# Expert stage of a diffusion block: each block's scatter-add is queued one iteration later on GpSimd, and the gathered rows are held in two tiles by column halves

## The chip, the cores and the metric

The program runs on one core of a Trainium2 chip. The metric is the device time of one execution in microseconds. TensorE does the matrix products, ScalarE and VectorE convert and scale, GpSimd issues the indirect DMAs (gather and scatter) and makes fp16 copies, SyncE issues the plain loads. In the profile they are called PE (PEld for its weight loads), ACT, DVE, POOL and SP.

## The reference, cut to what matters

One layer of a hybrid backbone: three groups of heads side by side (gated MLP, attention, gated recurrence), an output projection, and then a mixture of experts over 2048 tokens. Only the last part is touched here. Every token goes to two of 32 experts; an expert is a gated MLP with weights w1 and w3 (1024 x 512) and w2 (512 x 1024), and its output is added to the token's row, scaled by the token's gate:

```
out = (silu(xb @ w1[e]) * (xb @ w3[e])) @ w2[e]
x   = x + g2 * segment_sum(out[dest] * gate, token)
```

## The kernel before

`moe` (L1345 and on) works through 47 blocks of token rows. The experts are ranked by load; rank r has room for `CAPS[r]` groups of 64 rows, so a block is **full** (128 rows, 29 of them) or **half** (64 rows, 18 of them). The list `seq` takes a large, a middle and a small expert in turn, so the early part of the stage has more blocks per expert (more products for each weight loaded) than the late part.

The order of the instructions on PE, ACT, DVE and POOL is the order of the Python code (`manual_schedule`); each engine takes its own in order, and what is written first goes first. Iteration i does, in this order:

- `fetch(i + 4)`: on POOL, two small register loads and up to two loads of the index table (L1371, L1375).
- `gather(i + 2)`: on POOL, an indirect DMA that brings the rows of block i+2 into `xg` (L1443).
- first quarter of `gate_up(i)`: PE multiplies two 128-column chunks of x by w1 and w3, high part and residue (L1488, L1490) and then the fp16 weight residue (L1493 for half blocks, L1496 for full ones).
- `hidden(i - 1)`: PE transposes the activation `ac` of the block before into `pat` (L1469); ACT writes its rounded part `ah`, DVE the residue `al` (in `ah` itself for half blocks), POOL the fp16 copy `ab` (L1437).
- second quarter of `gate_up(i)`, then `rows(i + 1)`: PE transposes `xg` into the PSUM tile `pxt` (L1453), and twice, for columns 0 to 3 and 4 to 7 of the chunks, ACT writes `xh` (L82), DVE `xl` (L85; in `xh` for half blocks), POOL `xb` (L1437).
- third and fourth quarter of `gate_up(i)`, the activation (`sg`, `ac`), then `down(i - 1)`: PE multiplies `ah`, `al` by w2 (L1488, L1490) and `ab` by w2's residue (L1493, L1496) into `py`; ACT and DVE make `ysb`, the scaled output (L1544, L1545, L1547); POOL scatters it with an add into `out` (L1549).

The scatter is the last POOL instruction of an iteration, ahead of the next iteration's index load, gather and `ab`:

```
nc.gpsimd.indirect_dma_start(
    out=a["out"], out_offset=bass.IndirectOffsetOnAxis(ap=idx[r][:n, j, 0:1], axis=0),
    in_=y[:n], in_offset=None, compute_op=OP.add)
```

Between these steps the weights come in 384 pieces of 512 KB through five buffers `wstage` (L1406, on SP). ACT (L1416) makes the rounded part of a piece and DVE (L1417) its residue, which frees the buffer for the next load. `ahead` places these conversions by a fixed count of time for each quarter, so their place among the other ACT and DVE instructions is fixed in the program; up to 15 pieces of w1 and w3 and 7 of w2 lie ready ahead of PE. `ysb` has one buffer, `xg`, `xh`, `xl` and `xb` two, the index tile seven.

Of the kernel before, what the change touches and what calls it, by code (L numbers as in the profile page):

```python
# [10 lines left out]
F32 = mybir.dt.float32  # L11
F32R = mybir.dt.float32r
F16 = mybir.dt.float16
I32 = mybir.dt.int32
U8 = mybir.dt.uint8
AF = mybir.ActivationFunctionType
OP = mybir.AluOpType
# [4 lines left out]
P = 128  # L22
D = 1024
KT = D // P
# [50 lines left out]
class Kern:  # L75
# [1271 lines left out]
    def moe(self):  # L1347
        nc, tc, a = self.nc, self.tc, self.a
# [7 lines left out]
        seq = [(r, j) for r in order for j in range(nb(r))]  # L1356
        half = lambda r, j: 2 * j + 1 == CAPS[r]
        with ExitStack() as es:
            pool = es.enter_context(tc.tile_pool(name="moe", bufs=2, reuse_waits="tile"))
# [1 line left out]
            g2 = pool.tile([P, D], F32, name="g2", bufs=1)  # L1361
            nc.sync.dma_start(g2, self.mod_d[0:1, 5 * D:6 * D].to_broadcast([P, D]))
            nc.vector.tensor_scalar(g2, g2, 1.0 / UP, None, op0=OP.mult)
            idx, XG, XT, AC, AT, W = {}, {}, {}, {}, {}, {}

            def fetch_idx(r):
                e = nc.gpsimd.value_load(self.perm[0:1, r:r + 1], min_val=0, max_val=E_ - 1)
                n = CAPS[r] // 2
                t = pool.tile([P, 4, 2], I32, name="idx", bufs=7)
                if n:  # L1370
                    nc.gpsimd.dma_start(t[:, :n],  # L1371
                                        tabv[bass.ds(e, 1), :n * P].rearrange("o (j p) c -> p (o j) c", p=P))
                idx[r] = t
                if CAPS[r] % 2:
                    nc.gpsimd.dma_start(t[:64, n:n + 1], tabv[bass.ds(e, 1), n * P:n * P + 64]  # L1375
                                        .rearrange("o (j p) c -> p (o j) c", p=64))
# [24 lines left out]
            def pump():  # L1401
                p = next(gen, None)
                if p is None:
                    return
                st = pool.tile([P, 1024], F32, name="wstage", bufs=self.STG)
                nc.sync.dma_start(st if p[0][1] == "w2" else st.rearrange("p (k f) -> p k f", k=2), p[1])  # L1406
                dq.append((p[0], st))
# [13 lines left out]
            def need(r, w, k):  # L1421
                while (r, w, k) not in W:
                    split_next()
                    clock[0] = max(clock[0] - self.PACE, -self.PACE)
                return W[r, w, k]
# [3 lines left out]
            def ahead(t):  # L1429

                clock[0] = min(clock[0] + t, 3 * self.PACE)
                while clock[0] >= self.PACE and dq and free[kind(dq[0][0][1])] > 0:
                    split_next()
                    clock[0] -= self.PACE

            def half16(o, x):
                nc.gpsimd.tensor_scalar(o, x, -65504.0, 65504.0, op0=OP.max, op1=OP.min)  # L1437
# [9 lines left out]
            def rows(i):  # L1447

                n = 64 if half(*seq[i]) else P
                xg = XG.pop(i)  # L1450
                pt = ps.tile([P, KT, n], F32, name="pxt")
                for k in range(KT):
                    nc.tensor.transpose(pt[:, k], xg[:n, k * P:(k + 1) * P], self.ident[:n, :n])  # L1453
                h = pool.tile([P, KT, P], F32R, name="xh", bufs=2)
                l = h[:, :, 64:] if n == 64 else pool.tile([P, KT, P], F32R, name="xl", bufs=2)
                b = pool.tile([P, KT, P], F16, name="xb", bufs=2)
                for s in range(2):
                    ss = slice(4 * s, 4 * s + 4)
                    self.split(h[:, ss, :n], l[:, ss], pt[:, ss])
                    half16(b[:, ss, :n], h[:, ss, :n])  # L1460
                XT[i] = h, l, b

            def hidden(i):

                n = 64 if half(*seq[i]) else P
                ac = AC.pop(i)
                pt = ps.tile([P, 4, n], F32, name="pat")
                for k in range(4):
                    nc.tensor.transpose(pt[:, k], ac[:n, k * P:(k + 1) * P], self.ident[:n, :n])  # L1469
                h = pool.tile([P, 4, P], F32R, name="ah", bufs=1)  # L1470
                l = h[:, :, 64:] if n == 64 else pool.tile([P, 4, P], F32R, name="al", bufs=1)
                b = pool.tile([P, 4, P], F16, name="ab", bufs=1)
                self.split(h[:, :, :n], l, pt)
                half16(b[:, :, :n], h[:, :, :n])
                AT[i] = h, l, b

            def mm(i, out, x, ws, cs, last):


                small = half(*seq[i])  # L1480
                h, l, b = x
                first = small and (cs[0] // 2) % 2 == 1
                for low in ((True, False) if first else (False, True)):
                    for m, c in enumerate(cs):
                        for s in range(2):
                            w = ws[s][m][low]
                            if not low:
                                nc.tensor.matmul(out[s], h[:, c], w, start=(c == 0), stop=(first and c == last))  # L1488
                                if not small:
                                    nc.tensor.matmul(out[s], l[:, c], w, start=False, stop=False)  # L1490
                            elif small:
                                z = slice(64 * s, 64 * s + 64)
                                nc.tensor.matmul(out[s][z], b[:, c, :64], w, start=False, stop=False,  # L1493
                                                 tile_position=(0, 64 * s))
                            else:
                                nc.tensor.matmul(out[s], b[:, c], w, start=False, stop=(c == last))  # L1496

            def gate_up(i):

# [27 lines left out]
            def down(i):  # L1527
                r, j = seq[i]
                x = AT.pop(i)
                py = ps.tile([P, 2, 512], F32, name="py")  # L1530
                out = py[:, 0], py[:, 1]
                for k in (0, 2):
                    pcs = [need(r, "w2", k + m) for m in range(2)]
                    ws = [[[v[:, s * 512:(s + 1) * 512] for v in pc] for pc in pcs] for s in range(2)]
                    mm(i, out, x, ws, (k, k + 1), 3)
                    if j == nb(r) - 1:
                        free["w2"] += 2
                    ahead(6.5 if half(r, j) else 12)
                y = pool.tile([P, D], F32, name="ysb", bufs=1)
                src = pf = py.rearrange("p a b -> p (a b)")  # L1540
                n = P
                if half(r, j):
                    n = 64
                    nc.scalar.activation(y[:64], pf[64:], AF.Copy)  # L1544
                    nc.vector.tensor_tensor(y[:64], pf[:64], y[:64], op=OP.add)  # L1545
                    src = y
                nc.vector.scalar_tensor_tensor(y[:n], src[:n], idx[r][:n, j, 1:2].bitcast(F32), g2[:n],  # L1547
                                               op0=OP.mult, op1=OP.mult)
                nc.gpsimd.indirect_dma_start(  # L1549
                    out=a["out"], out_offset=bass.IndirectOffsetOnAxis(ap=idx[r][:n, j, 0:1], axis=0),  # L1550
                    in_=y[:n], in_offset=None, compute_op=OP.add)

            def fetch(i):
                if i < len(seq) and seq[i][1] == 0:
                    fetch_idx(seq[i][0])

            N = len(seq)
            with tc.manual_schedule(engines=ENGINES):
                for i in range(4):
                    fetch(i)  # L1560
                for _ in range(self.STG):
                    pump()
                gather(0)
                gather(1)
                rows(0)
                for i in range(N):
                    fetch(i + 4)
                    if i + 2 < N:
                        gather(i + 2)
                    g = gate_up(i)  # L1570
                    next(g)
                    if i:
                        hidden(i - 1)
                    next(g)
                    if i + 1 < N:
                        rows(i + 1)
                    for _ in g:
                        pass
                    if i:
                        down(i - 1)  # L1580
                hidden(N - 1)
                down(N - 1)
        self.overflow()

    def overflow(self):
# [151 lines left out]
```

## Time and profile before

| | us |
|---|---|
| median of 3 runs | 2933.82 |
| range of the runs | 2923.05 to 2935.71 |
| the profiled execution | 2931.78 |
| its span, first to last instruction | 2930.1 |
| expert stage in it, first weight load to last instruction | 2055 to 2930 |

The span is that of the program's own instructions; 1.7 us lie around it. Busy shares say how full an engine is, waits say what it stood for; a wait is told as "who <- whom", with its total, how often and the longest. `PEclk` is the granted TensorE clock: 1.0 is 2.4 GHz and 0.5 is 1.2 GHz.

### The profile page before, as it was taken

The page shows a single profiled execution, that of the slowest core. Times are in us where ns is not written, and L with a number is a line of the kernel's source. Part 1 is how long each engine was busy: PE and PEld are TensorE (multiplying, and loading weights), DVE is VectorE, ACT ScalarE, POOL GpSimd, SP SyncE. Part 2 cuts the span into 40 slices and gives each one's busy share as a digit, 9 for nine tenths or more (in the row PEclk, how much of TensorE's full clock was granted, in tenths as well). Part 3 has the DMA queues.
Part 4 walks back from the last instruction along what each step waited for, and adds up shares of the span by engine and source line. Part 5 has one row for each costly group of instructions (what it writes and reads, how often), then busy time and mean ns, then how long its engine had stood idle before and what let it go on. Part 6 is the DMA issues. An engine that isn't in the chain of part 4 may idle for free. (4 is left out here: it accounts for less than half of the span.)

```text
span 2930.1 us, 39701 instructions
## 1 busy us (share of the span) xinstructions
PE 2598.4 (89%) x13276; PEld 1918.9 (65%) x13276; DVE 2021.8 (69%) x3049; ACT 1547.4 (53%) x2599; POOL 1740.4 (59%) x1374
## 2 busy tenths in 40 slices
PE   6888888679978999999999999997798989898886
PEld 3778887568865666666666667776465555564553
DVE  3777767674445666667777654777678778878885
ACT  3344333312224777778887882222456656666664
POOL 3334333547775777778888885554455555555453
PEclk9999999789998999999999999998899999998998
DMA  7221223133321111121101006432789889999995
GB/s 283 95 78 65 80 87 105 46 104 99 103 81 60 60 58 50 57 67 34 31 30 30 17 10 200 151 131 76 268 264 285 281 265 308 307 299 290 290 296 156
DMA packets 208686, 409.99 MB, mean 140 GB/s; under 512 B 27568, under 2 KB 82224, under 8 KB 208352
## 3 DMA queue, kind: packets, MB, share of 16 engines
q1 hardware_dynamic: 194976, 367.52, 37.6%
q0 software_dynamic: 13504, 39.93, 6.3%
q8 instruction: 105, 1.72, 0.2%
q14 instruction: 101, 0.83, 0.1%
HBM read 336.00 MB, written 71.37 MB: 139 GB/s over the span
## 5 line engine op out<-in xcount | busy, mean ns | idle before, releaser
L963 POOL TENSOR_TENSOR pl<-pf,ph 128x512 f16<-128x512 f32 x512 | 683.9, 1345 | 155.9 <-ACT ph L960 131.8
L900 DVE TENSOR_REDUCE mx<-pmx 128x1 f32<-128x512 f32 (+1 forms) x640 | 403.3, 636 | 206.7 <-PE pmx L898 199.9
L959 ACT ACTIVATE pf<-s 128x512 f32<-128x512 f32 x576 | 344.5, 598 | 177.7 <-PE s L956 158.8
L1417 DVE SCALAR_TENSOR_TENSOR w13l<-wstage,w13h 128x1024 f16<-128x1024 f32 x256 | 319.1, 1279 | 35.3 <-ACT w13h L1416 30.7
L960 ACT ACTIVATE ph<-s 128x512 fp32r<-128x512 f32 x576 | 342.0, 594 | 0.0
L1549 POOL DMA_INDIRECT out_dram<-ysb,idx x47 | 117.4, 2499 | 365.7 <-DVE ysb L1547 357.8
L976 PE MATMUL p<-ph,one 128*128 128x512 f32 x576 | 333.1, 578 | 0.0
L1416 ACT ACTIVATE w13h<-wstage 128x1024 fp32r<-128x1024 f32 x256 | 261.5, 1051 | 90.6 <-DMA wstage<-in_w_dram 58.6
L1488 PE MATMUL ph<-w13h,xh 128*128 128x512 f32 x752 | 289.5, 431 | 20.1 <-DVE ac L1524 6.8
L898 PE MATMUL pmx<-k,q 128*128 128x512 f32 (+1 forms) x640 | 242.3, 380 | 8.1 <-DVE mx L900 3.9
L956 PE MATMUL s<-qB,kB 65*128 65x512 f32 x576 | 231.5, 402 | 6.4 <-POOL kB L947 6.4
L955 PE MATMUL s<-q,k 128*128 128x512 f32 x576 | 230.3, 400 | 0.0
L974 PE MATMUL p<-ph,VV 128*128 128x512 f32 x576 | 226.9, 394 | 0.0
L975 PE MATMUL p<-pl,V 128*128 128x512 f16 x576 | 224.2, 389 | 1.2 <-ACT ec L984 1.1
L1488 PEld LDWEIGHTS ph<-w13h,xh 128*128 128x128 f32 x752 | 139.5, 191 | 77.1 <-issue 15.4
L1490 PE MATMUL ph<-w13h,xl 128*128 128x512 f32 x464 | 184.9, 398 | 0.0
L536 PE MATMUL pa<-Q,kz 128*128 128x128 f32 x896 | 127.3, 302 | 62.4 <-DVE Asc L561 50.0
L1417 DVE SCALAR_TENSOR_TENSOR w2l<-wstage,w2h 128x1024 f16<-128x1024 f32 x128 | 158.3, 1262 | 30.3 <-ACT w2h L1416 20.7
L1437 POOL TENSOR_SCALAR xb<-xh 128x512 f16<-128x512 f32 (+1 forms) x94 | 168.1, 1819 | 15.9 <-ACT xh L82 15.9
L1488 PE MATMUL py<-w2h,ah 128*128 128x512 f32 x376 | 156.3, 463 | 10.5 <-ACT ah L82 5.3
L536 PEld LDWEIGHTS pa<-Q,kz 128*128 128x128 f32 x896 | 119.7, 214 | 68.7 <-issue 44.0
L975 PEld LDWEIGHTS <-V 128*128 128x128 f16 x576 | 54.9, 95 | 149.9 <-issue 139.2
(378 smaller groups left out, 6562.2 us busy)
## 6 DMA issues: line engine op xcount, KB each, us to landing
wstage<-in_w_dram SPq DMA_DIRECT2D x384, 512.0 KB
wm<-in_w_mod_dram SPq DMA_DIRECT2D x48, 512.0 KB
xtok<-in_x_tok_dram SPq DMA_DIRECT2D x34, 512.0 KB
hf<-h_d SPq DMA_DIRECT2D x19, 512.0 KB
xT<-in_xT_dram SPq DMA_DIRECT2D x18, 512.0 KB
h_d<-xT SPq DMA_DIRECT2D x18, 512.0 KB
qf<-qT_d SPq DMA_DIRECT2D x64, 128.0 KB
out_dram<-xn SPq DMA_DIRECT2D x16, 512.0 KB
```

The costliest lines, as they stand in the source:

```text
L536: nc.tensor.matmul(pa[:, hd], self.kz[l][:, hd, s], Q[:, hd, s], start=True, stop=True)
L898: nc.tensor.matmul(pm[:, :m], q2[:, t * P:(t + 1) * P], kk[:, j * 512:j * 512 + m], start=True, stop=True)
L900: nc.vector.tensor_reduce(mx[:, t, j:j + 1], pm[:, :m], axis=AX.X, op=OP.max)
L956: nc.tensor.matmul(s, kB[:, g, j], qB, start=False, stop=True)
L959: nc.scalar.activation(pf, s, AF.Exp, scale=0.125)
L960: nc.scalar.activation(ph, s, AF.Exp, scale=0.125)
L963: subs.append(lambda: e.tensor_tensor(pl, pf, ph, op=OP.subtract))
L975: nc.tensor.matmul(p[1], V1[:, g, j].rearrange("p s d -> p (s d)"), pl, **f)
L976: nc.tensor.matmul(p[1], one, ph, start=False, stop=(j == NT - 1))
L1416: nc.scalar.activation(h, st, AF.Copy, scale=UP)
L1417: nc.vector.scalar_tensor_tensor(l, st, UP, h, op0=OP.mult, op1=OP.subtract)
L1488: nc.tensor.matmul(out[s], h[:, c], w, start=(c == 0), stop=(first and c == last))
```

## The change

The scatter becomes a function of its own, `scatter(i)`. In iteration i, block i-2 is scattered, right after `hidden(i - 1)` and ahead of the second quarter of `gate_up(i)`; it was block i-1 at the end of the iteration. `ysb` gets two buffers and the index tile eight. `rows` makes for each half of the chunks its own tiles `xh`, `xl`, `xb` (four buffers of half the size), and `mm` takes chunk c from tile c // 4. The PSUM tile `pxt` stays one tile, and the order of ACT, DVE and PE instructions stays as it was.

```diff
-                t = pool.tile([P, 4, 2], I32, name="idx", bufs=7)
+                t = pool.tile([P, 4, 2], I32, name="idx", bufs=8)
...
-                h = pool.tile([P, KT, P], F32R, name="xh", bufs=2)
-                l = h[:, :, 64:] if n == 64 else pool.tile([P, KT, P], F32R, name="xl", bufs=2)
-                b = pool.tile([P, KT, P], F16, name="xb", bufs=2)
+                x = []
                 for s in range(2):
-                    ss = slice(4 * s, 4 * s + 4)
-                    self.split(h[:, ss, :n], l[:, ss], pt[:, ss])
-                    half16(b[:, ss, :n], h[:, ss, :n])
-                XT[i] = h, l, b
+                    h = pool.tile([P, 4, P], F32R, name="xh", bufs=4)
+                    l = h[:, :, 64:] if n == 64 else pool.tile([P, 4, P], F32R, name="xl", bufs=4)
+                    b = pool.tile([P, 4, P], F16, name="xb", bufs=4)
+                    self.split(h[:, :, :n], l, pt[:, 4 * s:4 * s + 4])
+                    half16(b[:, :, :n], h[:, :, :n])
+                    x.append((h, l, b))
+                XT[i] = x
...
-                y = pool.tile([P, D], F32, name="ysb", bufs=1)
+                y = pool.tile([P, D], F32, name="ysb", bufs=2)
...
+                Y[i] = y[:n]
+
+            def scatter(i):
+                r, j = seq[i]
+                y = Y.pop(i)
                 nc.gpsimd.indirect_dma_start(
...
                     if i:
                         hidden(i - 1)
+
+                    if i > 1:
+                        scatter(i - 2)
                     next(g)
...
                 hidden(N - 1)
+                scatter(N - 2)
                 down(N - 1)
+                scatter(N - 1)
```

## Rows read from the trace of the kernel before

**Rows 1.** The page: busy time of each engine over the whole span, and the busy share of the DMA engines in 40 equal slices.

```profile
PE 2598.4 (89%) x13276; PEld 1918.9 (65%) x13276; DVE 2021.8 (69%) x3049; ACT 1547.4 (53%) x2599; POOL 1740.4 (59%) x1374
DMA  7221223133321111121101006432789889999995
```

**Rows 2.** Busy time of each engine (and instructions) by stretch of the expert stage: the stretch and its length in us, then PE, PEld, DVE, ACT, POOL, the granted TensorE clock, the busy share of the DMA engines, and GB/s.

```profile
2100.00:2450.00 350.00, 323.09 (x1544) 207.51 (x1544) 273.57 (x276) 207.82 (x255) 197.05 (x115) 0.98 0.88 276
2450.00:2850.00 400.00, 350.22 (x1617) 219.83 (x1617) 328.61 (x324) 252.27 (x302) 209.93 (x126) 0.94 0.95 299
2850.00:2930.00 80.00, 52.74 (x239) 30.86 (x237) 49.16 (x52) 35.02 (x45) 31.46 (x19) 0.84 0.60 164
```

**Rows 3.** The same view in stretches of 50 us: the two with the highest DMA share.

```profile
2450.00:2500.00 50.00, 46.50 (x222) 29.68 (x221) 39.80 (x41) 30.55 (x38) 26.39 (x17) 0.97 0.97 312
2800.00:2850.00 50.00, 41.27 (x201) 25.06 (x198) 42.96 (x42) 33.14 (x40) 20.64 (x12) 0.96 0.97 303
```

**Rows 4.** The waits of the whole expert stage (2055 to 2930 us): who waited for whom, us in total, times, longest.

```profile
POOL out_dram L1549 <- DVE ysb L1547: 357.8, 46, 12.7
ACT xh L82 <- DVE xl L85: 60.4, 29, 3.7
ACT w13h L1416 <- DMA wstage<-in_w_dram: 58.6, 85, 2.5
...
PE py L1496 <- POOL ab L1437: 44.2, 19, 4.6
...
ACT w2h L1416 <- DMA wstage<-in_w_dram: 33.7, 51, 3.1
ACT xh L82 <- DVE xh L85: 33.5, 18, 2.9
...
ACT ysb L1544 <- DMA out_dram<-ysb,idx: 6.0, 2, 3.1
...
PE py L1493 <- POOL ab L1437: 5.7, 5, 2.6
PE ph L1488 <- ACT w13h L1416: 5.5, 2, 3.0
...
PEld L1493 <- POOL xb L1437: 1.5, 4, 0.4
PEld L1496 <- POOL xb L1437: 0.8, 3, 0.3
```

**Rows 5.** The same view for 2100 to 2450 us.

```profile
PE py L1496 <- POOL ab L1437: 18.4, 7, 4.5
PE py L1493 <- POOL ab L1437: 1.0, 1, 1.0
```

**Rows 6.** The same view for 2450 to 2850 us.

```profile
PE py L1496 <- POOL ab L1437: 23.5, 10, 4.6
PE py L1490 <- DVE al L85: 7.0, 3, 2.3
PE ph L1488 <- DVE ac L1524: 6.8, 6, 1.9
PE ph L1488 <- ACT sg L1523: 5.5, 3, 2.7
PE py L1488 <- ACT ah L82: 5.3, 3, 2.6
PE py L1493 <- POOL ab L1437: 3.0, 2, 2.6
```

**Rows 7.** The timeline of one iteration, from 2309 us on: start, length, engine, line, what it writes and reads, how many; in brackets the idle time before it and what ended it.

```profile
2310.60 0.60 ACT L82 ACTIVATE ah<-pat 128x512 fp32r<-128x512 f32 x1
...
2312.04 0.59 ACT L82 ACTIVATE xh<-pxt 128x512 fp32r<-128x512 f32 x1
...
2312.56 2.87 POOL L1549 DMA_INDIRECT out_dram<-ysb,idx  x1 [9.79 <-DVE ysb L1547]
...
2314.92 1.16 POOL L1371 DMA_DIRECT2D idx<-tab_d  x1
2315.08 0.67 DVE L85 TENSOR_TENSOR xl<-pxt,xh 128x512 fp32r<-128x512 f32 x1
...
2315.79 0.60 ACT L82 ACTIVATE xh<-pxt 128x512 fp32r<-128x512 f32 x1 [3.16 <-DVE xl L85]
...
2316.39 1.02 POOL L1443 DMA_INDIRECT xg<-h_d,idx  x1 [0.30 <-issue]
...
2317.43 2.94 POOL L1437 TENSOR_SCALAR ab<-ah 128x512 f16<-128x512 f32 x1
...
2320.35 4.88 POOL L1437 TENSOR_SCALAR xb<-xh 128x512 f16<-128x512 f32 x2
...
2320.43 1.89 PE L1496 MATMUL py<-w2l,ab 128*128 128x512 f16 x4 [4.46 <-POOL ab L1437]
```

**Rows 8.** Busy time by stretch again (columns as in rows 2), right behind that wait and after it.

```profile
2320.43:2323.40 2.97, 2.97 (x8) 1.78 (x9) 2.87 (x4) 1.29 (x2) 2.97 (x2) 0.50 1.03 392
2323.50:2326.90 3.40, 3.40 (x17) 2.36 (x16) 3.18 (x3) 2.93 (x4) 1.73 (x1) 1.00 0.80 294
```

**Rows 9.** The scatter's line: its instructions with shortest, median and longest in ns and first and last start in us, and the time from issue to landing.

```profile
L1549 POOLq EVENT_SEMAPHORE  x47: 17/17/43, 2097.8 to 2912.1; - x47
L1549 POOL DMA_INDIRECT out_dram<-ysb,idx x47: 1458/2362/6275, 2108.1 to 2917.9; - x47
DMA to landing us min/median/max: 4.7/9.1/11.7
```

**Rows 10.** POOL's instructions in the expert stage, kept apart by shape: busy us in all, mean ns of one, idle time before them.

```profile
L1437 POOL TENSOR_SCALAR xb<-xh 128x512 f16<-128x512 f32 x58 | 124.6, 2165 | 15.9 <-ACT xh L82 15.9
L1549 POOL DMA_INDIRECT out_dram<-ysb,idx x47 | 117.4, 2499 | 365.7 <-DVE ysb L1547 357.8 <-DVEq L1588 7.9
...
L1437 POOL TENSOR_SCALAR ab<-ah 128x512 f16<-128x512 f32 x29 | 69.4, 2394 | 8.2 <-ACT ah L82 7.5
```

**Rows 11.** POOL's timeline at the end of the stage.

```profile
2907.38 1.48 POOL L1549 DMA_INDIRECT out_dram<-ysb,idx  x1 [7.65 <-DVE ysb L1547]
2908.39 1.60 POOL L1437 TENSOR_SCALAR ab<-ah 128x256 f16<-128x256 f32 x1
2917.86 1.46 POOL L1549 DMA_INDIRECT out_dram<-ysb,idx  x1 [7.88 <-DVEq L1588]
```

More of the change, by code (lines that the diff above doesn't have):

```diff
@@ L1363, in moe @@
             nc.vector.tensor_scalar(g2, g2, 1.0 / UP, None, op0=OP.mult)
-            idx, XG, XT, AC, AT, W = {}, {}, {}, {}, {}, {}
+            idx, XG, XT, AC, AT, Y, W = {}, {}, {}, {}, {}, {}, {}
             def fetch_idx(r):
@@ L1474, in hidden @@
                 half16(b[:, :, :n], h[:, :, :n])
-                AT[i] = h, l, b
+                AT[i] = [(h, l, b)]
             def mm(i, out, x, ws, cs, last):
                 small = half(*seq[i])
-                h, l, b = x
                 first = small and (cs[0] // 2) % 2 == 1
@@ L1484, in mm @@
                     for m, c in enumerate(cs):
+                        h, l, b = (v[:, c % 4] for v in x[c // 4])
                         for s in range(2):
@@ L1487, in mm @@
                             if not low:
-                                nc.tensor.matmul(out[s], h[:, c], w, start=(c == 0), stop=(first and c == last))
+                                nc.tensor.matmul(out[s], h, w, start=(c == 0), stop=(first and c == last))
                                 if not small:
-                                    nc.tensor.matmul(out[s], l[:, c], w, start=False, stop=False)
+                                    nc.tensor.matmul(out[s], l, w, start=False, stop=False)
                             elif small:
                                 z = slice(64 * s, 64 * s + 64)
-                                nc.tensor.matmul(out[s][z], b[:, c, :64], w, start=False, stop=False,
+                                nc.tensor.matmul(out[s][z], b[:, :64], w, start=False, stop=False,
                                                  tile_position=(0, 64 * s))
                             else:
-                                nc.tensor.matmul(out[s], b[:, c], w, start=False, stop=(c == last))
+                                nc.tensor.matmul(out[s], b, w, start=False, stop=(c == last))
             def gate_up(i):
@@ L1548, in down @@
                                                op0=OP.mult, op1=OP.mult)
+                Y[i] = y[:n]
+            def scatter(i):
+                r, j = seq[i]
+                y = Y.pop(i)
                 nc.gpsimd.indirect_dma_start(
-                    out=a["out"], out_offset=bass.IndirectOffsetOnAxis(ap=idx[r][:n, j, 0:1], axis=0),
-                    in_=y[:n], in_offset=None, compute_op=OP.add)
+                    out=a["out"], out_offset=bass.IndirectOffsetOnAxis(ap=idx[r][:y.shape[0], j, 0:1], axis=0),
+                    in_=y, in_offset=None, compute_op=OP.add)
             def fetch(i):
```

## The prediction

> **What bounds the kernel now.** I read the page first: the DMA engines are nearly full in the last third of the span, which is the expert stage [rows 1]. Then the busy time by stretch [rows 2]. From 2100 to 2450 us PE is busy 323.09 of 350 us with the DMA share at 0.88; from 2450 to 2850 us PE is busy 350.22 of 400 us with the share at 0.95, and the two fullest stretches of 50 us stand at 0.97 [rows 3]. So PE sets the pace of the early part, and in the late part the loads are within a few per cent of the most that this run shows. DVE is no reserve either: 328.61 of 400 us. Third, the waits [rows 4]. The longest, 357.8 us of POOL for `ysb`, costs nothing by itself; what matters is who stands behind POOL. PE stands 44.2 + 5.7 = 49.9 us for `ab`, POOL's fp16 copy. PE's wait for converted weights is 5.5 us in two places, so it is never short of weights for long; the loads bite elsewhere, on ACT (58.6 + 33.7 = 92.3 us).
>
> The timeline of one iteration [rows 7] shows the mechanism. `ah` is written by 2310.60 + 0.60 = 2311.20. POOL is then held by the scatter, which waited 9.79 us for `ysb` and issues from 2312.56 for 2.87 us; index load (1.16 us) and gather (1.02 us) come next, and `ab` starts only at 2317.43, 6.2 us after `ah` was there. It ends at 2320.37, and PE, which had come to its use 4.46 us earlier, goes on at 2320.43. Behind such a wait PE runs at the lower clock level: 8 matmuls in 2.97 us at 0.50 (1.2 GHz), against 17 in 3.40 us at 1.00 (2.4 GHz) afterwards [rows 8].
>
> **The change, part by part.** *Scatter.* Nothing is removed; 47 scatters of 2.36 us median [rows 9] go from ahead of index load, gather and `ab` to behind `ab`. `ysb` of block i-2 is written at the end of iteration i-1, so POOL no longer stands for it, and index load and gather are issued at the start of an iteration; they bring their transfers some microseconds forward, still one block each per iteration. In the iteration shown `ab` could start at 2311.2 and end at 2314.1 (2.94 us), before PE wants it. I put the 49.9 us at zero afterwards.
>
> By stretch: early 18.4 + 1.0 = 19.4 us [rows 5], late 23.5 + 3.0 = 26.5 us [rows 6], the rest (4.0 us) at the ends. To this comes the clock. One long wait costs 8 x (2.97/8 - 3.40/17) = 1.4 us [rows 8]. From above: a granted mean of 0.98 over 350 us means 14 us at half clock, a loss of 7 us; 0.94 over 400 us means 48 us, a loss of 24 us [rows 2]. The `ab` waits are nearly all of the long ones early, but only about half late (26.5 us beside 7.0 + 6.8 + 5.5 + 5.3 = 24.6 us of other waits [rows 6]). So I take 5 us early and 12 us late. PE alone would give 24 us early and 38 us late.
>
> Now what is late next. **Early**, 24 us less raise the DMA share to 0.88 x 350/326 = 0.945, the level that the late part holds, so the loads allow it. But PE then comes sooner to `al`, `ac`, `sg` and `ah`, whose makers ACT and DVE keep their order; I give a third back, 8 us: 16 us. **Late**, the loads allow less: if the share can rise from 0.95 to the 0.97 of rows 3, 400 x (1 - 0.95/0.97) = 8 us; if to 1.00, 20 us; nothing, if 0.95 is what this mix holds. I take 8 us, since 0.97 is a level seen twice. **At the end** [rows 11] the copy `ab` of the last block and ACT's wait for the single `ysb` buffer (6.0 us in two places [rows 4]) go, up to 6 us. But a scatter also waits for a semaphore ahead of it (47 of them [rows 9]), which I read as the landing of the one before, and landing takes 9.1 us; the last two scatters are 10.5 us apart now, so the last can come forward little: between 0 and 6 us I take 3.
>
> *Behind the moved scatter* on POOL now stands `xb` of block i+1. `xb` was ready in time before (PE's weight loads waited 1.5 + 0.8 us [rows 4]). In the iteration shown the old order ended `xb` at 2325.23; the new one would run `ab` to 2314.1, scatter to 2317.0, `xb` to 2321.9 at the same lengths: earlier, since the 9.79 us wait no longer sits in front. Zero, with the third rival as its other end. The second `ysb` buffer adds no wait: block i is written in iteration i+1, a whole iteration after the scatter of block i-2 was issued, and an iteration (first to last scatter, 809.8 us, over 46: 17.6 us) is longer than the longest landing, 11.7 us [rows 9]. SP gets no new instruction and nothing passes its queue.
>
> *x in two tiles.* No instruction is added: the same two conversions by each engine. The wait that it might remove is ACT's, for the second half of `xh`: 60.4 + 33.5 = 93.9 us [rows 4]. I cost it at zero, and the reason is in rows 7. ACT's second `xh` starts at 2315.79, as DVE's first `xl` ends (2315.75); POOL's `xb` reads the same columns of `xh` as `xl` did and comes ahead of that ACT instruction in the code, yet runs only at 2320.35. Had ACT waited for readers of the whole `xh` tile, it would have waited for POOL too. What only ACT and DVE share is `pxt`, which stays one tile. From both sides: nothing, or at most what PE loses to late ACT and DVE work in the late part, 24.6 us [rows 6].
>
> The Trainium skill (PSUM — Partial Sum Buffer, section on bank collisions) says that a dependency is put between two engines' accesses to one 2 KiB PSUM bank, reads included. By it the wait of the 18 half blocks (33.5 us) comes from `pxt`, whose halves then share a bank; the halves of a full block fill a bank each, so that its 60.4 us would need another source, the x tile, and the second rival, with its 2887 us, would gain weight. The rows agree on the half blocks and speak for `pxt` on the full ones too.
>
> **Sum.** 16 early + 8 late + 3 at the end = 27 us. The profiled execution (2931.78; span 2930.1) would be 2904.8; it lies 2 us below the median of 2933.82, so the median would be about 2906.
>
> **Rivals.** *The loads take it back.* The late part already holds 0.95, and a faster PE early only meets ACT and DVE sooner; then late gains nothing and early a third, about 8 us: 2926. For it: ACT's 92.3 us on loads, and DVE at 82% late. Against it: PE's waits for `ab` are there whether or not the loads are full, and up to 22 pieces lie ready ahead.
>
> *The x halves free ACT as well.* If the 93.9 us go, ACT reaches `sg` and `ah` about 2 us earlier in each block, and DVE `al` and `ac`. Early the 8 us given back stay won, and late the loads allow 20 us rather than 8: 27 + 8 + 12 = 47 us, 2887.
>
> *`xb` comes late: slower.* In each iteration the scatter now stands between `ab` and `xb`. If PE came to `xb` with no slack, all 117.4 us of scatter (47 of 2.5 us [rows 10]) would lie on the path, less the 49.9 us won: 67 us longer, 3001. It decides where POOL's `ab` (2.39 us), scatter and two `xb` (2.17 us each [rows 10]) together end after PE has finished `down(i-1)`; that sum is 9.2 us. PE has more: `gate_up` is two thirds of a block's products, so the quarter of it ahead of `hidden` is a sixth of 17.6 us, and about 14.7 us are left for the rest. So it needs half blocks that pass quickly, or scatters near their longest, 6.3 us [rows 9].
>
> **How the numbers follow.** A measurement of this kernel can tell about 0.5%, 14.7 us, from no change. Chances: forecast (15 to 40 us gained) 0.60, loads take it back 0.23, x halves free ACT 0.09, `xb` late 0.08. Faster 0.69, same 0.23, slower 0.08. The range reaches up to the second case's near-nothing, 2932, and down to 2876: all of PE's 24 us early, 20 us late and 6 us at the end are 50 us, and some of the x halves' share (8 us).
>
> **What would show it.** After the change, PE's waits for `ab` near zero and POOL's wait for `ysb` far below 357.8 us; `ab` starting within 1 us of `ah`; DMA share early near 0.94, late 0.96 to 0.97; granted clock late above 0.94; ACT's waits `xh` <- `xl`/`xh` still near 94 us. Wrong if `ab` still waits, if PE waits for `xb`, if the late stretch shortens by far more than 8 us, or if ACT's `xh` waits fall away.

## The result, and the profile after

| | before | after |
|---|---|---|
| median of 8 runs each, us | 2925.99 | 2896.53 |
| range, us | 2913.8 to 2935.71 | 2892.44 to 2903.8 |
| ratio, 95% interval | | 0.9902 (0.9881 to 0.9924) |
| profiled execution, span, us | 2930.1 | 2892.9 |
| block 0 to 21 / 21 to 42 / 42 to 46, us | 365.7 / 392.6 / 51.5 | 344.9 / 384.9 / 44.1 |

The change makes the kernel 29.5 us faster by the medians (1.0%); 27 us were forecast, 2906 us with a range from 2876 to 2932. The two profiled executions differ by more, 37.2 us, because that of before (2931.78 us) lies near the upper end of its runs and that of after (2894.6 us) near the lower end. One execution of e11 (below) was slow, 5038.69 us, and stands in no ratio. Against the 2906 us forecast, 2896.53 lies 9.5 us lower, and 7.8 of these are the kernel before itself, whose median came down from 2933.82 with more runs. The last row splits the stage by work done instead of by time: from the moment at which DVE has finished `ysb` of one block to that of a later block. The early part gives 20.8 us, the late part 7.7, the end 7.4. These add up to 35.9 us: they belong to the 37.2 us between the two executions, not to the 29.5. How firm such a part is can be seen from four kernels below that keep POOL's old order and the add (e2, e3, e11, e12): they take 363 to 373 us early and 389 to 394 us late, so several us of a part can be chance.

In the changed kernel the lines have moved: products L1489 (high part), L1491 (residue), L1494 and L1497 (weight residue), scatter L1555, `sg` L1519 to L1524, `ac` L1520 to L1525.

First the waits of the expert stage, who for whom, us in total, times, longest. They answer to [rows 4] and [rows 6].

```profile
POOL ab L1437 <- ACT ah L82: 328.8, 47, 12.6
ACT w13h L1416 <- DMA wstage<-in_w_dram: 86.3, 72, 4.4
ACT xh L82 <- DVE xl L85: 54.3, 29, 3.6
...
ACT w2h L1416 <- DMA wstage<-in_w_dram: 34.6, 48, 3.8
...
ACT xh L82 <- DVE xh L85: 29.6, 18, 2.4
...
PE ph L1489 <- DVE sg L1519: 23.3, 14, 2.7
...
PE ph L1489 <- ACT sg L1524: 12.2, 7, 3.0
...
PE py L1491 <- DVE al L85: 9.0, 4, 2.8
...
POOL out_dram L1555 <- DVE ysb L1548: 2.4, 3, 1.3
...
PE ph L1494 <- POOL xb L1437: 0.3, 1, 0.3
```

POOL's long wait has changed its owner: 357.8 us of the scatter for `ysb` have become 2.4, and POOL now stands 328.8 us ahead of `ab`, once a block, for ACT's `ah`. There the wait harms little: what is queued behind it, the scatter and `xb`, is not missed by PE (0.3 us for `xb`). PE's 49.9 us for `ab` are gone from its rows. What grew is PE's wait for `sg`, from 1.6 + 6.0 us to 23.3 + 12.2 us: the next block's first product needs the PSUM tile that ACT and DVE are still reading.

One iteration's POOL and ACT rows (start, length) answer to [rows 7]: `ab` starts 0.10 us after `ah` has ended, where it was 6.2 us.

```profile
2301.17 0.60 ACT L82 ACTIVATE ah<-pat 128x512 fp32r<-128x512 f32 x1
...
2301.87 2.79 POOL L1437 TENSOR_SCALAR ab<-ah 128x512 f16<-128x512 f32 x1 [6.37 <-ACT ah L82]
```

Busy time between the end of block 0's `ysb` and that of block 21, and on to block 42 (columns as in [rows 2]); first the kernel before, then after.

```profile
2107.80:2473.50 365.70, 338.79 (x1631) 217.29 (x1629) 286.66 (x289) 220.63 (x269) 205.71 (x120) 0.98 0.89 279
2473.50:2866.10 392.60, 341.51 (x1563) 214.22 (x1560) 325.00 (x322) 248.87 (x299) 209.23 (x124) 0.93 0.95 297
```

```profile
2106.60:2451.50 344.90, 332.55 (x1615) 212.59 (x1614) 287.30 (x288) 216.74 (x266) 202.54 (x121) 0.99 0.94 297
2451.50:2836.40 384.90, 342.13 (x1580) 211.88 (x1579) 322.83 (x321) 248.81 (x301) 201.36 (x123) 0.94 0.96 305
```

The work is the same, and most busy times hardly move; PE's falls early by 6.2 us (4.1 in e8, the full change again), with the granted clock up from 0.98 to 0.99. PE's idle time early falls from 365.70 - 338.79 = 26.9 us to 12.4 us, and late from 51.1 us only to 42.8 us. The DMA share rises from 0.89 to 0.94 and from 0.95 to 0.96.

And the tail, POOL's last rows, which answer to [rows 11], with DVE's last:

```profile
2869.57 1.06 POOL L1437 TENSOR_SCALAR ab<-ah 128x256 f16<-128x256 f32 x1 [3.60 <-ACT ah L82]
...
2871.91 1.48 POOL L1555 DMA_INDIRECT out_dram<-ysb,idx  x1 [1.28 <-DVE ysb L1548]
...
2879.22 1.28 DVE L1548 SCALAR_TENSOR_TENSOR ysb<-ysb,idx,g 64x1024 f32<-64x1024 f32 x1
2880.78 1.43 POOL L1555 DMA_INDIRECT out_dram<-ysb,idx  x1 [7.39 <-DVEq L1599]
```

The last two scatters stand 8.9 us apart, where they stood 10.5. The first of the two landed 4.7 us after its issue, so by about 2876.6; the last one starts at 2880.78, just after DVE has ended its `ysb` at 2880.50.

### The profile page after: what moved, and what is told of

Its sections match the earlier page's. It is cut to its first block, busy times and chain, and to the rows that moved or that the text cites. A ratio compares the mean times of both kernels' runs of the same rounds, so it can differ in the third digit from the quotient of the medians.

```text
span 2892.9 us, 39700 instructions
## 1 busy us (share of the span) xinstructions
PE 2589.7 (90%) x13276; PEld 1911.1 (66%) x13276; DVE 2016.2 (70%) x3049; ACT 1543.7 (53%) x2599; POOL 1729.2 (60%) x1374
## 5 line engine op out<-in xcount | busy, mean ns | idle before, releaser
L1489 PE MATMUL ph<-w13h,xh 128*128 128x512 f32 x752 | 291.1, 433 | 46.2 <-DVE sg L1519 23.3
L1437 POOL TENSOR_SCALAR ab<-ah 128x512 f16<-128x512 f32 (+1 forms) x47 | 104.1, 2214 | 328.8 <-ACT ah L82 328.8
L1489 PEld LDWEIGHTS ph<-w13h,xh 128*128 128x128 f32 x752 | 140.1, 192 | 112.1 <-DVE sg L1519 31.5
L1437 POOL TENSOR_SCALAR xb<-xh 128x512 f16<-128x512 f32 (+1 forms) x94 | 185.0, 2184 | 17.4 <-ACT xh L82 17.4
L1491 PE MATMUL ph<-w13h,xl 128*128 128x512 f32 x464 | 186.6, 402 | 0.0
L1489 PE MATMUL py<-w2h,ah 128*128 128x512 f32 x376 | 147.4, 439 | 11.2 <-ACT ah L82 5.7
```

The costliest lines, as they stand in the source:

```text
L1489: nc.tensor.matmul(out[s], h, w, start=(c == 0), stop=(first and c == last))
```

## The experiments

The theory: on POOL, `ab` was queued behind a scatter that waited for `ysb`; PE waited for `ab`; moving the scatter ends that, early it turns into time, late the loads of weights swallow most of it, and the x halves do nothing. Rivals: the x halves free ACT; the early gather is what helps; the single `ysb` buffer was the stall. Runs of one group of four share a chip and the runs of the kernel before on it (medians 2930.5, 2928.75 and 2928.37 us). Gains below are told from the ratio unless a median is named; the ratio is not the quotient of the two medians, and the two ways differ by up to some 4 us (e1, e3).

| run | median, us | ratio to before, 95% interval |
|---|---|---|
| e1, scatter moved alone | 2897.52 | 0.9873 (0.9852 to 0.9894) |
| e2, x halves alone | 2926.26 | 0.9983 (0.9969 to 0.9996) |
| e3, buffers alone | 2922.93 | 0.9959 (0.9943 to 0.9975) |
| e4, scatter just ahead of `ab` | 2893.91 | 0.9865 (0.9846 to 0.9885) |
| e5, full change, `pxt` in two tiles | 2877.91 | 0.9833 (0.9811 to 0.9855) |
| e6, old scatter, gather behind `ab` | 2900.76 | 0.9904 (0.9886 to 0.9922) |
| e7, full change, no add | 2867.58 | 0.9798 (0.9777 to 0.9818) |
| e8, full change again | 2898.11 | 0.9892 (0.9876 to 0.9908) |
| e9, before, no add | 2887.04 | 0.9861 (0.9837 to 0.9885) |
| e10, scatter moved, x whole, `pxt` in two | 2878.45 | 0.9825 (0.9797 to 0.9852) |
| e11, before, `pxt` in two | 2926.13 | 1.0001 (0.9983 to 1.0019) |
| e12, before, two `ysb` buffers | 2926.32 | 0.9997 (0.9982 to 1.0011) |

**e1: the scatter alone.** The changed kernel with the old `rows` and `mm`.

```diff
-                x = []
...
+                h = pool.tile([P, KT, P], F32R, name="xh", bufs=2)
+                l = h[:, :, 64:] if n == 64 else pool.tile([P, KT, P], F32R, name="xl", bufs=2)
+                b = pool.tile([P, KT, P], F16, name="xb", bufs=2)
```

> The scatter is moved (with its second ysb buffer and eighth index buffer), x stays in one tile per part as before. Theory (POOL's copy ab stood behind the scatter; the x halves do nothing): the whole gain is here, 29 us faster than before (22 to 37), PE's waits for ab zero. Rival (the x halves free ACT and carry part of the gain): at least 8 us less gain than the full change, so 21 us or less.

Measured: 33 us better by the medians, 37 by the ratio (31 to 43), and no wait of PE for `ab` has a row any more. The full change gained 29.5 and 32 us in its two groups, so its whole gain is in the scatter and the two buffers that go with it.

**e2: the x halves alone.** The kernel before with the new `rows` and `mm`.

> x in two tiles alone, the scatter where it was. Theory: no change (within 5 us of before); ACT's waits of its second xh for DVE stay near 94 us and PE's waits for ab near 50 us. Rival (the halves free ACT): 8 to 20 us faster, and those waits fall below 40 us.

Measured: 5 us by the ratio (1 to 9), and the waits did not fall:

```profile
ACT xh L82 <- DVE xl L85: 66.6, 29, 3.8
...
PE py L1497 <- POOL ab L1437: 47.8, 18, 4.5
ACT xh L82 <- DVE xh L85: 33.4, 18, 2.8
```

ACT still stands 100.0 us, so the wait does not come from the x tile. PE's waits for `ab`, with those of the half blocks, are 60.0 us. The 5 us have no mechanism in these rows; e1 and e10, which do without the halves and lose nothing, put them in doubt.

**e3: the buffers alone.**

```diff
-                t = pool.tile([P, 4, 2], I32, name="idx", bufs=7)
+                t = pool.tile([P, 4, 2], I32, name="idx", bufs=8)
...
-                y = pool.tile([P, D], F32, name="ysb", bufs=1)
+                y = pool.tile([P, D], F32, name="ysb", bufs=2)
```

> Old order of the instructions, but ysb with two buffers and the index tile with eight. Theory (order on POOL is what counts; the single ysb buffer costs only at the end, 6.0 us in two waits): 0 to 6 us faster, PE's waits for ab still near 50 us. Rival (the single ysb buffer holds up the scatter chain all along): 15 us faster or more, ab waits halved.

Measured: 12 us (7 to 17) better by the ratio, 7.6 by the medians, between the two expectations and twice the upper end of the theory's. PE's waits for `ab` are not shorter (48.1 + 9.8 us), which speaks against the scatter chain. Its profiled execution took 2932.33 us, the longest of its nine, and shows no gain anywhere; it cannot say where the others found theirs.

**e12: the `ysb` buffer without the index buffer**, asked because of e3.

> The kernel before with two ysb buffers alone (index tile at seven). Theory: 0 to 6 us better, all at the end of the stage. Rival (the 12 us of the earlier run with both buffers came from ysb): 8 to 16 us better.

Measured: no change (from 5 us faster to 3 us slower). So e3's 12 us do not come from `ysb`; whether the eighth index buffer brings them, or another place of the tiles in SBUF, or the chip, stays open. It matters for the sum: if the 12 us are real, the buffers carry that much of the gain of e1 and e6, and the order on POOL the rest.

**e4: the scatter of block i-2 just ahead of `hidden(i-1)`.**

```diff
-                    if i:
-                        hidden(i - 1)
-
                     if i > 1:
                         scatter(i - 2)
+                    if i:
+                        hidden(i - 1)
```

> The full change, but the scatter of block i-2 stands just ahead of hidden(i-1) instead of just behind it: index load and gather are past POOL's wait for ysb, only ab still stands behind the scatter. Theory (ab's start decides): ab starts when ysb and 2.4 us of scatter are through, so about 2.2 us (index load and gather) sooner than before and still 3 to 4 us later than in the full change; waits of PE for ab fall from 50 us to 10 to 25 us, and the time is 10 to 20 us better than before. Rival (the early gather and index load are what helps): the full 29 us.

The waits came as expected, 14.1 + 2.8 us, the time did not: 40 us better (34 to 45), as good as e1 beside it (37). Either the early gather was the helper, or the last third of the waits for `ab` costs nothing.

```profile
POOL out_dram L1555 <- DVE ysb L1548: 313.5, 46, 11.7
...
PE py L1497 <- POOL ab L1437: 14.1, 10, 2.6
...
PE py L1494 <- POOL ab L1437: 2.8, 3, 1.2
```

Its late part took 375.3 us, 8 to 12 less than with the scatter behind `ab` (383.6 in e1, 384.9 and 387.0 in the full change), at a DMA share of 0.97 and a clock of 0.96. So the last waits for `ab` do not set the late part; what shortened it there is not shown, and one execution of each is all there is.

**e6: only the order of gather and `ab` changed**, on the kernel of e3. The scatter stays last of the iteration; index load and gather go behind `ab`, so the gather now comes later than in the kernel before.

```diff
-                    fetch(i + 4)
-                    if i + 2 < N:
-                        gather(i + 2)
                     g = gate_up(i)
                     next(g)
                     if i:
                         hidden(i - 1)
+                    fetch(i + 4)
+                    if i + 2 < N:
+                        gather(i + 2)
```

> The kernel before with two ysb and eight index buffers, the scatter where it was (last of the iteration), but index load and gather moved behind ab: of what stood ahead of ab only the scatter is left, and the gather comes later than before instead of sooner. Theory (the time at which ab starts is what counts): as with the scatter just ahead of ab, PE's waits for ab fall to about 17 us and the time is 30 to 37 us better than before. Rival (the early gather is what helps): no better than the buffers alone, 0 to 12 us.

Measured: 28 us better (23 to 33), a little under the 30 to 37 expected; the waits for `ab` are short:

```profile
PE py L1496 <- POOL ab L1437: 9.3, 8, 1.5
...
PE py L1493 <- POOL ab L1437: 1.6, 2, 1.3
```

A late gather does not undo the gain, so the early one is not its cause. The moment at which `ab` starts decides, and not down to zero: with 11 to 17 us of waits left (e6, e4) the time cannot be told from that of the full change. The early part took 353.9 us here, between before and after.

**e8: the full change again**, for the comparisons of its group.

> The full change once more, on the chip of the three others: 28 to 37 us better than before (0.987 to 0.990).

Measured: 0.9892, 32 us (27 to 36). Its parts are 346.6 / 387.0 / 45.3 us; the first two (columns as in [rows 2]):

```profile
2106.90:2453.50 346.60, 334.73 (x1615) 213.54 (x1614) 289.56 (x287) 216.49 (x266) 203.21 (x121) 0.99 0.94 295
2453.50:2840.50 387.00, 346.04 (x1580) 214.51 (x1579) 322.57 (x321) 249.28 (x301) 201.40 (x123) 0.93 0.95 304
```

**e5: `pxt` in two PSUM tiles**, on the full change.

```diff
-                pt = ps.tile([P, KT, n], F32, name="pxt")
+                pt = [ps.tile([P, 4, n], F32, name=f"pxt{s}") for s in range(2)]
                 for k in range(KT):
-                    nc.tensor.transpose(pt[:, k], xg[:n, k * P:(k + 1) * P], self.ident[:n, :n])
+                    nc.tensor.transpose(pt[k // 4][:, k % 4], xg[:n, k * P:(k + 1) * P], self.ident[:n, :n])
...
-                    self.split(h[:, :, :n], l, pt[:, 4 * s:4 * s + 4])
+                    self.split(h[:, :, :n], l, pt[s])
```

> The full change, and the PSUM tile pxt made two tiles of four chunks each. Theory (ACT's second xh waits for DVE's first xl because both read the one tile pxt): ACT's waits xh <- xl and xh <- xh, 84 us in the full change, fall below 30 us. Rival (they come from the x tile or from DVE's queue): they stay near 84 us. Time: 0 to 8 us better than the full change, since ACT comes earlier to sg and ah but the loads are nearly full.

ACT's waits for DVE's `xl` and `xh`, 56.3 + 33.0 us in e8, have no row any more; its two `xh` run back to back (start, length):

```profile
2295.32 0.60 ACT L82 ACTIVATE ah<-pat 128x512 fp32r<-128x512 f32 x1
...
2296.77 1.07 ACT L82 ACTIVATE xh<-pxt 128x512 fp32r<-128x512 f32 x2
```

The time is 20.2 us better than e8 by the medians, more than twice the upper end of what I gave it, and e5 and e10 are the fastest kernels here that leave nothing out. By blocks (columns as in [rows 2]) 7 us come early and 14.5 us late, where the DMA share rises from 0.95 to 0.98:

```profile
2106.10:2445.60 339.50, 331.43 (x1615) 213.34 (x1614) 287.62 (x289) 216.86 (x268) 217.24 (x121) 0.99 0.94 300
2445.60:2818.10 372.50, 338.45 (x1580) 211.02 (x1579) 320.31 (x321) 247.53 (x299) 205.84 (x123) 0.95 0.98 315
```

So in the full change the late part was held not by the DMA engines alone but also by ACT's waits for DVE: freed of them, ACT comes sooner to the pieces (its waits for loads grow from 114.9 us in e8 to 139.5) and to `sg` (PE's waits for `sg` fall from 27.6 + 6.2 us to 11.6 + 9.1).

**e10: the same with x in one tile** (e1 with `pxt` in two).

> The scatter moved and pxt in two tiles, x in one tile per part. Theory (the x halves do nothing): as with x in halves, 47 to 52 us better than before, ACT's waits of its second xh for DVE gone. Rival (with pxt split the x halves begin to matter): those waits come back in part (30 us or more) and the gain is 40 us or less.

Measured: 0.9825, 51 us (43 to 59), like e5's 49 us (42 to 55), and the waits stay gone. The x halves do nothing with the split `pxt` either.

**e11: `pxt` in two with the scatter where it was.**

> The kernel before with pxt in two tiles alone, the scatter where it was. If the two stalls are separate, 20 us better, as on top of the moved scatter. If PE's waits for ab (POOL behind the scatter) swallow what ACT gains, 0 to 8 us.

Measured: nothing, 1.0001 (from 5 us faster to 6 us slower). ACT's waits for `xl` and `xh` are gone here too, but PE stands for `ab` as before:

```profile
PE py L1496 <- POOL ab L1437: 44.3, 14, 7.1
...
PE py L1493 <- POOL ab L1437: 6.0, 6, 1.8
```

The two stalls are not separate: as long as POOL's queue sets the start of `ab`, freeing ACT is worth nothing. That ACT's gain only brings PE sooner to `ab` is argued and not shown: the waits for `ab` did not grow (50.3 against 49.9 us). What grew is ACT's wait, at `sg`, for PE's products, from 40.1 to 83.0 us: ACT is early and PE is not.

**e7 and e9: the scatters write without adding**, on the full change and on the kernel before.

```diff
-                    in_=y, in_offset=None, compute_op=OP.add)
+                    in_=y, in_offset=None)
```

> The full change, with the add left out of the 47 scatters (a plain write). If the DMA engines bound the late part now, their share drops and the late part (block 21 to 42, 385 us) shortens by 5 to 15 us. If PE, DVE and ACT bound it, within 3 us of the full change.

> The kernel before, with the add left out of the 47 scatters. In the full change this took 20 us off the late part and nothing off the early one. Theory (before the change PE's waits for ab set the pace early, loads and waits together late): early part within 4 us, late part 5 to 15 us shorter, 8 to 18 us in all, so less than the 30 us in the full change. Rival (the loads bound the late part before just as much): 25 us or more.

e7: 30.5 us better than e8 by the medians, more than expected. In the profiled executions the early part takes 345.6 against 346.6 us, no change, the late one 367.3 against 387.0 us. That execution of e7 was the slowest of its five (2879.76 us, median 2867.58), so these parts show less than the medians do. e9: 41 us better than before (34 to 48), where I expected 8 to 18; the rival has it. Early 347.7 against 365.7 us, late 369.4 against 392.6 us. The windows of e7 and then of e9 (columns as in [rows 2]), the waits of e9 for `ab`, and its scatter's row (busy us, mean ns):

```profile
2108.50:2454.10 345.60, 334.60 (x1615) 214.43 (x1614) 284.47 (x288) 217.21 (x268) 189.69 (x121) 0.98 0.86 297
2454.10:2821.40 367.30, 332.97 (x1581) 206.04 (x1579) 318.02 (x321) 248.32 (x301) 193.84 (x123) 0.98 0.93 320
```

```profile
2107.20:2454.90 347.70, 332.86 (x1617) 213.51 (x1616) 287.38 (x288) 217.89 (x269) 184.25 (x120) 0.99 0.87 294
2454.90:2824.30 369.40, 330.59 (x1575) 206.95 (x1574) 319.94 (x322) 248.45 (x298) 198.21 (x124) 0.98 0.94 316
```

```profile
PE py L1496 <- POOL ab L1437: 27.4, 13, 2.9
...
PE py L1493 <- POOL ab L1437: 6.0, 9, 1.3
...
L1549 POOL DMA_INDIRECT out_dram<-ysb,idx x47 | 82.9, 1764 | 354.5 <-DVE ysb L1547 346.7 <-DVEq L1588 7.9
```

The add is dear. Without it the scatter's instruction falls from 2.50 us [rows 10] to 1.76 us, the DMA engines move 316 instead of 297 GB/s late, ACT's waits for loads fall from 92.3 to 79.5 us. Much of what it gives late is TensorE's clock: the granted share there is 0.98 in e7 and e9 against 0.93 in e8 and before, and PE's busy time falls by 13.1 us in e7 and by 10.9 in e9. The early part is helped as well, to 347.7 us, near the 345 to 347 of the kernels with the scatter behind or just ahead of `ab`: PE is busy 333 us there, and waits for `ab` of 10 us are left. By the profiled executions the two cures hardly add, e9 and e7 being alike in both parts. The medians say otherwise: 31 us for the moved scatter (e8), 41 for the missing add (e9), 61 for both (e7), so they overlap by some 11 us of 72. That lighter DMAs shorten the waits for `ab` by way of an earlier `ysb` fits these rows, but no run isolates it.

## Why the prediction was right

**The mechanism held, link by link.** POOL's wait for `ysb` fell to 2.4 us, `ab` follows `ah` at once, PE's waits for `ab` went to zero, `xb` did not come late (0.3 us on PE). e1 puts the whole gain on the moved scatter with its buffers, e6 comes to 28 us by another order with the scatter left in place, and e12 finds nothing in the `ysb` buffer alone; what e3's 12 us were stays open. The forecast of 27 us lies inside the measured 22 to 35. That it meets 29.5 so closely is in part luck: the sum was made for the profiled execution, and between the profiled executions the gain was 37.2 us, and 31.9 us with e8's execution as that of after.

**Early: 16 us forecast, 20.8 and 19.1 us measured** (profiled execution and e8). Of the 19.4 us of `ab` waits 5.0 came back as other waits of PE, not 8: `al`, `ac`, `sg` together rose from 7.2 to 12.2 us. For the clock 5 us were set down, and PE's busy time fell by 6.2 and 4.1 us. So the terms are the right ones, and the third that I gave back was somewhat too much.

**Late: 8 us forecast, 7.7 and 5.6 measured, the reason half right.** I took the DMA share as the lid (0.95 to 0.97). It rose only to 0.96 and 0.95. And the removed waits, 24.8 + 3.0 us, came back on PE as waits for `sg` (13.6 + 9.2), `al` (8.1), `ah` (5.7 + 1.8) and `ac` (4.0 us): 42.4 us where 22.7 us had been, so 19.7 of 27.8 us. The rows of after between 2451.5 and 2836.4 us (who for whom, us, times, longest):

```profile
ACT w13h L1416 <- DMA wstage<-in_w_dram: 59.3, 45, 4.4
...
ACT w2h L1416 <- DMA wstage<-in_w_dram: 18.5, 25, 3.8
...
PE ph L1489 <- DVE sg L1519: 13.6, 9, 2.7
...
PE ph L1489 <- ACT sg L1524: 9.2, 5, 3.0
...
PE py L1491 <- DVE al L85: 8.1, 3, 2.8
...
PE py L1489 <- ACT ah L82: 5.7, 2, 3.9
...
PE ph L1489 <- DVE ac L1525: 4.0, 5, 1.1
...
PE py L1489 <- DVE ah L85: 1.8, 1, 1.8
```

The makers of these are ACT and DVE, and ACT's waits for loads grew to 77.8 us there from 53.9. Neither limit holds this part alone: lighter scatters took 19.7 us off it (e7 against e8), 13.1 of them PE's busy time, and freeing ACT took 14.5 us off (e5), with the share at 0.98. The 12 us that I set down for a better clock late did not come: 0.93 became 0.94 (0.93 in e8), and PE's busy time did not fall, 341.51 against 342.13 us. A clock above 0.94 was one of the announced signs, and it is missing.

**The end: 3 us forecast, 7.4 and 6.2 measured.** The mis-sized step is the bound by the scatter's landing: I took the median of all scatters, 9.1 us, but at the end landing is shorter: the last but one landed in 4.7 us, before the change as after it. The last scatter waited for DVE's `ysb`, not for that landing, and already so before, where it started at 2917.86 [rows 11] and `ysb` had ended at 2917.58. So the whole upper end of 6 us came. In e12, with the second `ysb` buffer alone, the end took 48.5 us against 51.5.

**x halves: zero.** e1 and e10 do as well without them; only e2's 5 us (1 to 9) stand against it. The cause of ACT's wait is the one argued: one PSUM tile `pxt` read by both engines (e2 and e5). The Trainium skill's rule (PSUM — Partial Sum Buffer, on bank collisions) would have put only the half blocks' waits on `pxt`, because the halves of a full block fill a bank each. Here the measurement decides: splitting the tile took away the 29 waits of full blocks too (56.3 us in e8), so in this kernel they were set per PSUM tile and not per bank.

**The rivals.** "The loads take it back" came near in the late part (7.7 and 5.6 us gained of the 38 that PE alone would give) and was wrong for the rest; that it was the loads alone is not so, as e5 shows. "The x halves free ACT" named the wrong edit but a real price: with ACT's waits gone by e5's edit the gain over before is 51 us (2928.75 to 2877.91), where I had worked out 47. "`xb` late" did not happen.

## What to carry to other kernels

An instruction that waits on an in-order queue costs what stands behind it: look for the engine's long wait, then for who waits for the instructions queued after it, and move the waiter behind them. Stalls in series hide each other (e11 nothing, e5 20 us for the same edit), so an edit that once failed may be tried again after another stall is gone. Splitting a tile helps where the engines really share it, here the PSUM tile and not the SBUF tiles.

## What was not expected of the hardware

The add in the scatter takes DMA time beyond its bytes. The queue that carries the gathers, the scatters and the index loads, before and in e9 (packets, MB, share of the 16 engines' span):

```profile
q0 software_dynamic: 13504, 39.93, 6.3%
```

```profile
q0 software_dynamic: 13504, 39.93, 3.9%
```

With the same packets and bytes, the scatter's median landing fell from 9.1 to 6.6 us, and the kernel before gained 41 us (34 to 48) of its 2928 when the add was left out.
